# One triangular substitution for a whole pair of heads, and 36 adaLN columns moved from VectorE to GpSimd and ScalarE

## The chip, the cores and the metric

The kernel runs on one core of one Trainium2 chip. The time is device time in microseconds (us), the median of three runs: 2511.28 before (2510.93 to 2513.99). Engines are named as the profile names them: PE (TensorE), PEld (its weight loads), DVE (VectorE), ACT (ScalarE), POOL (GpSimd), SP (SyncE, which issues all transfers here). Each engine has its own list of instructions, in the order in which they were built; semaphores make one engine wait for another.

## What is computed

One decoder layer in float32, batch 1, 512 tokens, width 2048:

```python
mod = silu(c) @ w_ada + b_ada            # 6 x 2048 values: shift, scale, gate of both sub-layers
h = modulate(rms_norm(x), sh_m, sc_m)
p = h @ w_in                             # RG-LRU part, its gate, RWKV part
y_a = rg_lru(conv(p_lru)) * gelu(p_gate)
y_b = rwkv7_mix(p_rwkv)                  # 16 heads of 64; state (64 x 64) per head over all tokens
x = x + g_m * (concat(y_a, y_b) @ w_out)
h = modulate(rms_norm(x), sh_f, sc_f)
x = x + g_f * ((silu(gate) * up) @ w_down)
return rms_norm(x)
```

The RWKV recurrence is worked in 8 chunks of 64 tokens for 8 pairs of heads. Within a chunk it needs, per head, the inverse of a unit triangular 64 x 64 matrix I - A.

## The kernel before

Large products are made of three float32r products each, of operands split into a high and a low part (lines 124 to 126, tiles `whi`, `wlo` of the weights and `hhi`, `hlo` or `yhi`, `ylo` of the activations). A block of weights comes in by SP, ACT casts it to `whi` (L105), DVE makes `wlo` (L106).

The mixing sub-layer is one long stage in which `weave` writes the order of work down once, when the program is built. It has streams of small dependent steps and a `filler` of large products (input projections of later pairs, the RG-LRU, and half of the output projection). It goes by a clock of its own: a stream's next step is placed when its stated latency has passed and what it needs has been placed; else three large products of the filler are placed. What PE does while it waits for a chain of small steps is therefore fixed beforehand, and if the filler is used up, nothing is placed between. The streams, by priority, are

- `chains`: for each pair, 8 chunks one after the other. A chunk's steps are a product (L694, L696), ACT's copy `rw_w` (L698), a product with the inverse `bd_xt` (L701), ACT's copy `rw_u` (L703), products L708 to L713, and DVE's next state `rw_s` (L720). After 8 chunks come group norm and gate (L729 to L745) and a store of the pair's `y`.
- `halves(0)`, `halves(1)`: four chunks of a pair. Operands, products within chunks (L633, L643), DVE's `rw_gb` and `rw_dg` (L635 to L639), transposes on PE (L655), and then `inverse` for these four chunks. A half of pair p is placed once four, or all eight, chunks of pair p-1 are placed.
- `mains`: what a pair needs of all tokens. `mods`: the adaLN columns 32 to 67.

`inverse` does a substitution by DVE in the diagonal 32 x 32 blocks. A transpose spreads `rw_dg` over the partitions (L757, tile `rw_at`), then 31 steps of a multiply (L764, `rw_xp`) and an add (L766, `rw_x`), each on the one before, then two transposes (L768 `rw_xn`, L771 `rw_xs`), and POOL's copies into `bd_xt` (L775). PE then makes the lower left blocks (L783, a copy by ACT, L793). `weave` counts 30.2 us for the substitution. The two halves of a pair have buffers of their own and may be under way together.

`mod_steps` makes an adaLN column in four quarters: SP loads 128 x 512 of `w_ada` (tile `adaq`, two buffers), and one DVE instruction multiplies by the spread silu(c) (`cbq`) and sums along the row (L199).

After the mixing, `channel` loads the eight `y` of the pairs back (`yraw`, two buffers), splits them (`yhi`, `ylo`), and runs the other half of the output projection.

Of the kernel before, what the change touches and what calls it, by code (L numbers as in the profile page):

```python
# [67 lines left out]
def _constants():  # L68
# [9 lines left out]
    r = ((p % 32) // 4)[:, None, None]  # L78
    con[:, _COFF["xinit"]:][:, :P] = (
        np.arange(32)[None, :, None] == 8 * np.arange(4)[None, None, :] + r).reshape(P, P)  # L80
# [965 lines left out]
```

## Time and profile before

| | before |
|---|---|
| median of 3 runs | 2511.28 us |
| span of the profiled execution | 2515.8 us (4.5 above the median; the page gives no other time of it) |
| busy: PE, DVE, ACT, POOL | 2413.9, 1380.4, 843.7, 82.0 us |
| 150 to 850 us (most of the mixing): PE, DVE, ACT busy of 700 | 667.9, 612.9, 374.8 us |
| mean granted PE clock | 0.986 |

The busy time of an engine over the whole span says little here, since the mixing and the later stages have different limits. A stage is read by its window; a wait is read by the pair of engines and lines that it names.

### The profile page before, as it was taken

What the parts mean: (1) busy time and instruction counts of PE and PEld (TensorE: products, weight loads), DVE (VectorE), ACT (ScalarE), POOL (GpSimd) and SP (SyncE); (2) the same over time, 40 slices, a digit from 0 to 9 for tenths busy, and PEclk for the clock granted to TensorE, in tenths of its full rate; (3) what the DMA queues carried; (4) which work ended last, traced back from release to release, by engine and by line L of the source; (5) the groups of instructions that cost most, each with busy time, mean ns of one, the idle gap of its engine ahead of it and who ended that gap; (6) DMA issues with size and microseconds to landing.
All of it is one profiled execution on the core that took longest, in us unless ns stands there. A gap on an engine that the chain in (4) does not pass through costs nothing.

```text
span 2515.8 us, 30983 instructions
## 1 busy us (share of the span) xinstructions
PE 2413.9 (96%) x11560; PEld 1953.4 (78%) x11560; DVE 1380.4 (55%) x3111; ACT 843.7 (34%) x1340; POOL 82.0 (3%) x131
## 2 busy tenths in 40 slices
PE   5999999999999999899999999999999999999997
PEld 3677777877777886687788888888888888888885
DVE  7979898999969847854423322233322233222244
ACT  4357364455355333432222222222222222222221
POOL 0000111111101000000000000000000000000000
PEclk9999998999999999999999999999999999999998
DMA  8864444444342438366423332323333233333233
GB/s 304 308 219 130 148 128 143 131 152 144 125 135 81 143 108 283 119 195 194 160 90 95 108 100 93 101 83 98 106 98 99 89 92 105 101 93 100 85 95 112
DMA packets 138938, 333.22 MB, mean 132 GB/s; under 512 B 15458, under 2 KB 28898, under 8 KB 134690
## 3 DMA queue, kind: packets, MB, share of 16 engines
q1 hardware_dynamic: 138788, 331.25, 40.7%
q8 instruction: 90, 1.47, 0.2%
q14 instruction: 60, 0.49, 0.1%
HBM read 322.92 MB, written 7.87 MB: 131 GB/s over the span
## 4 chain that ended last, share of the span: by engine, by line
PE 72%; DVE 9%; DMA 7%; issue 1%; ACT 1%; SPq 0%; POOL 0%; DVEq 0%; ACTq 0%
PE ps_mm L124 10%; PE ps_mm L126 10%; PE ps_mm L125 10%; PE ps_gr L126 6%; PE ps_st L124 6%; PE ps_gr L124 6%; PE ps_st L126 6%; PE ps_gr L125 6%; PE ps_st L125 6%; DMA adaq<-in_w_ada 6%; DVE adaq L199 2%; DVE wlo L106 2%; DVE rw_xp L764 1%; DVE rw_x L766 1%; DMA wraw<-in_w_out 1%
## 5 line engine op out<-in xcount | busy, mean ns | idle before, releaser
L106 DVE TENSOR_TENSOR wlo<-wraw,whi 128x1024 fp32r<-128x1024 f32 (+2 forms) x552 | 496.7, 902 | 730.2 <-ACT whi L105 721.1
L105 ACT CAST whi<-wraw 128x1024 fp32r<-128x1024 f32 (+2 forms) x552 | 436.6, 792 | 1292.4 <-PE ps_mm L125 401.1
L124 PE MATMUL ps_mm<-hhi,whi 128*128 128x512 f32 x1020 | 417.1, 410 | 9.8 <-ACT hhi L251 7.2
L126 PE MATMUL ps_mm<-hhi,wlo 128*128 128x512 f32 x1020 | 407.2, 399 | 1.7 <-DVE wlo L106 1.6
L125 PE MATMUL ps_mm<-hlo,whi 128*128 128x512 f32 x1020 | 406.5, 399 | 0.8 <-DVE hlo L252 0.7
L124 PEld LDWEIGHTS ps_mm<-hhi,whi 128*128 128x128 f32 x1020 | 193.4, 190 | 53.2 <-ACT hhi L251 9.9
L125 PEld LDWEIGHTS ps_mm<-hlo,whi 128*128 128x128 f32 x1020 | 193.7, 190 | 43.4 <-DVE hlo L252 4.8
L126 PEld LDWEIGHTS ps_mm<-hhi,wlo 128*128 128x128 f32 x1020 | 193.8, 190 | 42.3 <-DVE wlo L106 3.0
L199 DVE SCALAR_TENSOR_TENSOR adaq<-adaq,cbq 128x512 f32<-128x512 f32 x256 | 173.5, 687 | 92.9 <-DMA adaq<-in_w_ada 85.1
L126 PE MATMUL ps_gr<-hhi,wlo 128*128 128x512 f32 x496 | 193.7, 390 | 3.1 <-DVE wlo L106 3.1
L126 PE MATMUL ps_st<-hhi,wlo 128*128 128x512 f32 x496 | 193.6, 390 | 2.0 <-DVE wlo L106 2.0
L124 PE MATMUL ps_st<-hhi,whi 128*128 128x512 f32 x496 | 194.0, 391 | 1.6 <-ACT hhi L251 1.6
L125 PE MATMUL ps_gr<-hlo,whi 128*128 128x512 f32 x496 | 193.5, 390 | 0.0
L125 PE MATMUL ps_st<-hlo,whi 128*128 128x512 f32 x496 | 193.5, 390 | 0.0
L124 PE MATMUL ps_gr<-hhi,whi 128*128 128x512 f32 x496 | 192.6, 391 | 0.0
L126 PEld LDWEIGHTS ps_gr<-hhi,wlo 128*128 128x128 f32 x496 | 93.4, 188 | 23.6 <-DVE wlo L106 4.1
L126 PEld LDWEIGHTS ps_st<-hhi,wlo 128*128 128x128 f32 x496 | 93.4, 188 | 21.8 <-DVE wlo L106 2.5
L124 PEld LDWEIGHTS ps_st<-hhi,whi 128*128 128x128 f32 x496 | 93.5, 188 | 21.6 <-ACT hhi L251 2.2
L125 PEld LDWEIGHTS ps_gr<-hlo,whi 128*128 128x128 f32 x496 | 93.7, 189 | 19.6
L124 PEld LDWEIGHTS ps_gr<-hhi,whi 128*128 128x128 f32 x496 | 93.7, 189 | 19.4
L125 PEld LDWEIGHTS ps_st<-hlo,whi 128*128 128x128 f32 x496 | 93.3, 188 | 19.8 <-DVE hlo L252 0.3
L766 DVE TENSOR_TENSOR rw_x<-rw_x,rw_xp 128x27 f32<-128x27 f32 (+23 forms) x496 | 94.7, 196 | 5.7
(312 smaller groups left out, 3809.6 us busy)
## 6 DMA issues: line engine op xcount, KB each, us to landing
wraw<-in_w_gu SPq DMA_DIRECT2D x176, 512.0 KB, 3.6
adaq<-in_w_ada SPq DMA_DIRECT2D x256, 256.0 KB, 3.3
wraw<-in_w_in SPq DMA_DIRECT2D x160, 256.0 KB, 3.0
ada<-in_w_ada SPq DMA_DIRECT2D x32, 1024.0 KB, 7.2
wraw<-in_w_down SPq DMA_DIRECT2D x64, 512.0 KB, 3.5
wraw<-in_w_out SPq DMA_DIRECT2D x64, 256.0 KB, 3.3
wraw<-in_w_down SPq DMA_DIRECT2D x64, 192.0 KB, 2.3
x<-in_x SPq DMA_DIRECT2D x32, 256.0 KB, 5.3
```

The lines of the kernel that those rows point to most:

```text
L105: nc.scalar.copy(out=hi, in_=src)
L106: nc.vector.tensor_tensor(out=lo, in0=src, in1=hi.bitcast(F32), op=ALU.subtract)
L124: mm(ps, lhsT=w[0], rhs=x[0], start=start, stop=False)
L125: mm(ps, lhsT=w[0], rhs=x[1], start=False, stop=False)
L126: self.pe = mm(ps, lhsT=w[1], rhs=x[0], start=False, stop=stop).ins
L199: nc.vector.scalar_tensor_tensor(out=t, in0=t, scalar=1.0, in1=cb, op0=ALU.mult, op1=ALU.mult, accum_out=part[:, m, h:h + 1])
L764: tt(out=pr[:, :n, :j], in0=at[:, s + 1:, s:s + 1].to_broadcast([P, n, j]), in1=x[:, s:s + 1, :j].to_broadcast([P, n, j]), op=ALU.mult)
L766: tt(out=x[:, s + 1:, :j], in0=x[:, s + 1:, :j], in1=pr[:, :n, :j], op=ALU.add)
```

## The change

Per pair there is now one substitution for all eight chunks, in a stream `inverses` of its own, placed when both halves of the pair are built; its tiles hold twice the columns, and there is one buffer of each. `weave` counts 24.0 us for it. The chain of a pair starts when that one inverse is placed. The adaLN columns 32 to 67 (144 quarters) go through `mod_steps_pool`: POOL multiplies (L224), ACT sums along the row one quarter later (L215), and `adaq` has three buffers. Comments were taken out, which shifts the line numbers.

```diff
-INVLAT = 30.2                   # substitution in the diagonal blocks
+INVLAT = 24.0
...
+    def mod_steps_pool(self, js, pool, tags):
+        nc = self.nc
+        n = len(js)
+        part = self.small.tile([P, n, 4], F32, tag="adaparts", name="adaparts", bufs=1)
+        old = None
+
+        def total(t, at):
+            nc.scalar.activation(out=t, in_=t, func=AF.Copy, accum_out=at)
+
+        for h in range(4):
+            sl = slice(h * S, (h + 1) * S)
+            cb = pool.tile([P, S], F32, tag=tags[0], name="cbq", bufs=tags[1])
+            nc.sync.dma_start(out=cb, in_=self.csilu[:, sl].to_broadcast([P, S]))
+            for m, j in enumerate(js):
+                t = pool.tile([P, S], F32, tag=tags[2], name="adaq", bufs=tags[3])
+                nc.sync.dma_start(out=t, in_=self.i["w_ada"][j, :, sl])
+                nc.gpsimd.tensor_tensor(out=t, in0=t, in1=cb, op=ALU.mult)
+                if old is not None:
+                    total(*old)
+                old = t, part[:, m, h:h + 1]
+                yield
+        total(*old)
...
-                for _ in self.mod_steps(range(j, min(j + 16, 64 + 4)), self.rw, ("cbq", 1, "adaq", 2)):
+                for _ in self.mod_steps_pool(range(j, min(j + 16, 64 + 4)), self.rw, ("cbq", 1, "adaq", 3)):
...
+        def inverses():
+            for pr in range(NPAIR):
+                yield 0, 0, lambda: done["built"] == 2 * pr + 2
+                yield from self.inverse(*self.pairs[pr][-1])
+
         def chains():
             for pr in range(NPAIR):
-                yield 0, 0, lambda: done["inv"] > 2 * pr
+                yield 0, 0, lambda: done["inv"] > pr
                 yield from self.rwkv_chain(pr)
...
-        self.weave([chains(), halves(0), halves(1), mains(), mods()], self.filler)
+        self.weave([chains(), inverses(), halves(0), halves(1), mains(), mods()], self.filler)
...
-            if c == 4:
-                yield 0, 0, lambda: self.done["inv"] >= 2 * pr + 2
...
-        yield from self.inverse(hf, d, gb)
...
-        at = rw.tile([P, 32, 32], F32, tag=f"at{hf}", name="rw_at")
+        at = rw.tile([P, 32, 32], F32, tag="at", name="rw_at")
...
-        x = rw.tile([P, 32, 4], F32, tag=f"x{hf}", name="rw_x")
+        x = rw.tile([P, 32, 8], F32, tag="x", name="rw_x")
...
-            n, j = 31 - s, s // 8 + 1
+            n, j = 31 - s, s // 4 + 1
             tt(out=pr[:, :n, :j], in0=at[:, s + 1:, s:s + 1].to_broadcast([P, n, j]),
```

What now stands where, by the built order of both programs:

On PE, the place of the last substitution that PE uses. Before, in pair 7's second half (L783 is the product that takes `rw_xn`; `ps_mm<-yhi` are large products of the filler):

```order
L712 MATMUL ps_y<-rw_ar,rw_s 128x64
L713 MATMUL ps_y<-rw_gb,rw_u 128x64
L783 MATMUL ps_gr<-rw_xn,rw_gb 32x32 x8
L124 MATMUL ps_mm<-yhi,whi 128x512
L125 MATMUL ps_mm<-ylo,whi 128x512
L126 MATMUL ps_mm<-yhi,wlo 128x512
```

In the change (L783 is now L816, L793 is L826, the transposes L655 are L690, the chain's L701 and L709 are L733 and L741):

```order
L126 MATMUL ps_mm<-yhi,wlo 128x512
L657 MATMUL ps_st<-cons,mix_v 64x64 x8
L666 MATMUL ps_gr<-rw_ar,bd_b_1390 128x128 x4
L678 MATMUL ps_gr<-rw_ar,bd_k_1392 128x128 x4
L775 MATMUL ps_ch<-lora_g,rw_lwg 128x512
L776 MATMUL ps_ch<-lora_s,rw_lws 128x512
L690 MATMUL ps_st<-cons,bd_b_1390 128x128 x4
L726 MATMUL ps_ch<-bd_v_1402,bd_bt_1398 128x128
L690 MATMUL ps_st<-cons,bd_k_1392 128x128 x4
L742 MATMUL ps_y<-rw_rkt,bd_v_1402 128x64
L816 MATMUL ps_gr<-rw_xn,rw_gb 32x32 x16
L826 MATMUL ps_gr<-rw_xs,rw_rt 32x32 x16
```

The first of these rows is the filler's last product. From there to the end of pair 7's chain and its group norm no large product stands on PE; before, 273 of them stood between the last transposes L655 and the end of the filler, and the chain of pair 7 had ended 39 before it. Between the second half's last transposes and the substitution's first use, PE has 125, 116, 133, 112, 130, 123, 130 and 0 large products for pairs 0 to 7 (before, for the 16 halves, 96 to 181); on DVE there stand 101 to 111 rows of the order from the last `rw_dg` to `rw_xn` for pairs 0 to 6, of which 62 are the substitution and 9 to 12 are `wlo`.

On POOL, pair 2's second half to pair 2's copies of the inverse (L616 is now L649, L775 is L807). Before, with nothing else between:

```order
L616 TENSOR_SCALAR bd_a_1394<-rw_ar 64x4x64 x2
L775 TENSOR_SCALAR bd_xt_1407<-rw_xs 32x4x32 x4
L616 TENSOR_SCALAR bd_a_1395<-rw_ar 64x4x64 x2
L554 MEMSET rw_pb 128x8
L775 TENSOR_SCALAR bd_xt_1406<-rw_xs 32x4x32 x4
```

In the change:

```order
L649 TENSOR_SCALAR bd_a_1394<-rw_ar 64x4x64 x2
L224 TENSOR_TENSOR adaq<-adaq,cbq 128x512 x16
L649 TENSOR_SCALAR bd_a_1395<-rw_ar 64x4x64 x2
L587 MEMSET rw_pb 128x8
L224 TENSOR_TENSOR adaq<-adaq,cbq 128x512 x25
L807 TENSOR_SCALAR bd_xt_1406<-rw_xs 32x4x32 x4
L807 TENSOR_SCALAR bd_xt_1407<-rw_xs 32x4x32 x4
```

In the same stretch of pairs 0, 1 and 3 there are 18, 16 and 12 of these multiplies, and from pair 4 on none.

On ACT, from pair 7's last square (`L729`, now `L761`) to the projection. Before:

```order
L729 ACTIVATE rw_t_9389<-ps_y 128x512
L105 CAST whi<-wraw 128x512 x2
L735 ACTIVATE rw_t_9434<-ps_ch,eps 128x512
L736 ACTIVATE rw_t_9389<-rw_t_9434 128x512
L105 CAST whi<-wraw 128x512 x4
L105 CAST yhi<-yraw 128x512 x2
L105 CAST whi<-wraw 128x512
```

In the change:

```order
L761 ACTIVATE rw_t_9018<-ps_y 128x512
L767 ACTIVATE rw_t_9022<-ps_ch,eps 128x512
L768 ACTIVATE rw_t_9018<-rw_t_9022 128x512
L105 CAST yhi<-yraw 128x512 x4
L105 CAST whi<-wraw 128x512 x2
L105 CAST yhi<-yraw 128x512 x4
```

The casts of filler weights are gone from between, and the first weights that the projection needs are cast behind four `yhi`.

More of the change, by code (lines that the diff above doesn't have):

```diff
@@ L77, in _constants @@
     con[:, _COFF["gmask"] + C:][:, :C] = s <= t
[L78 to L80 removed]
+    r = ((p % 32) // 8)[:, None, None]
+    con[:, _COFF["xinit"]:][:, :256] = (
+        np.arange(32)[None, :, None] == 4 * np.arange(8)[None, None, :] + r).reshape(P, 256)
     q = (p // 32) % 2
@@ L201, in mod_steps @@
                 yield
+        dst = self.mod[:, js[0]:js[0] + n]
+        nc.vector.tensor_reduce(out=dst, in_=part, op=ALU.add, axis=AX.X)
+        o = _VOFF["b_ada"] + js[0]
+        nc.vector.tensor_tensor(out=dst, in0=dst, in1=self.vecs[:, o:o + n], op=ALU.add)
+    def mod_steps_pool(self, js, pool, tags):
[18 more added lines that the diff above has]
+        total(*old)
         dst = self.mod[:, js[0]:js[0] + n]
@@ L635, in rwkv_half @@
         tt(out=gb, in0=pv, in1=gm.unsqueeze(1).to_broadcast([P, 4, P]), op=ALU.mult)
-        d = rw.tile([P, 4, 32], F32, tag=f"dg{hf}", name="rw_dg")
+        if hf == 0:
+            parts.append(rw.tile([P, NCH, 32], F32, tag="dg", name="rw_dg"))
+        d = parts[0][:, 4 * hf:4 * hf + 4]
         nc.vector.tensor_scalar(out=d, in0=gb[:, :, 0:32], scalar1=self.m01[:, 0:1], scalar2=None,
@@ L748, in rwkv_chain, with inverse @@
         yield 1.07, 2.0, None
-    def inverse(self, hf, dg, gb):
+    def inverse(self, dg, *parts):
         nc, rw = self.nc, self.rw
@@ L766, in inverse @@
             tt(out=x[:, s + 1:, :j], in0=x[:, s + 1:, :j], in1=pr[:, :n, :j], op=ALU.add)
-        xn = rw.tile([P, 32, 4], F32, tag=f"at{hf}", name="rw_xn")
-        nc.vector.transpose(out=xn.rearrange("p (j r) c -> p j (r c)", r=8),
+        xn = rw.tile([P, 32, NCH], F32, tag="at", name="rw_xn")
+        nc.vector.transpose(out=xn.rearrange("p (j r) c -> p j (r c)", r=4),
                             in_=x.rearrange("p t j -> p j t"))
-        xs = rw.tile([P, 4, 32], F32, tag=f"dg{hf}", name="rw_xs")
+        xs = rw.tile([P, NCH, 32], F32, tag="xp", name="rw_xs")
         nc.vector.transpose(out=xs, in_=xn.rearrange("p j c -> p c j"))
-        xt = self.bd["xt"][hf]
-        for g in range(4):
-            rows = slice(g * 32, g * 32 + 32)
-            nc.gpsimd.tensor_scalar(out=xt[rows, :, rows], in0=xs[rows], scalar1=1.0,
-                                    scalar2=None, op0=ALU.mult)
+        for hf in range(2):
+            for g in range(4):
+                rows = slice(g * 32, g * 32 + 32)
+                nc.gpsimd.tensor_scalar(out=self.bd["xt"][hf][rows, :, rows], in0=xs[rows, 4 * hf:4 * hf + 4],
+                                        scalar1=1.0, scalar2=None, op0=ALU.mult)
         yield 0, INVLAT, None
-        ps = self.ps("gr").rearrange("p (c x) -> p c x", x=P)
-        for c in range(4):
+        ps = self.ps("gr").rearrange("p (c x) -> p c x", x=C)
+        for c in range(NCH):
+            gb = parts[c // 4][1]
             for g in range(2):
                 q0, q1 = slice(g * C, g * C + 32), slice(g * C + 32, g * C + C)
-                mm(ps[q1, c, :32], lhsT=gb[q0, c, 32:C], rhs=xn[q0, :, c], start=True, stop=True)
-        rt = rw.tile([P, 4, 32], F32, tag=f"x{hf}", name="rw_rt")
+                mm(ps[q1, c, :32], lhsT=gb[q0, c % 4, 32:C], rhs=xn[q0, :, c], start=True, stop=True)
+        rt = rw.tile([P, NCH, 32], F32, tag="x", name="rw_rt")
         for g in range(2):
@@ L787, in inverse @@
             nc.scalar.copy(out=rt[q1], in_=ps[q1, :, :32])
-        yield 0.43, HOP, None
-        ps = self.ps("gr").rearrange("p (c x) -> p c x", x=P)
-        for c in range(4):
+        yield 0.86, HOP, None
+        ps = self.ps("gr").rearrange("p (c x) -> p c x", x=C)
+        for c in range(NCH):
             for g in range(2):
@@ L793, in inverse @@
                 mm(ps[q0, c, :32], lhsT=rt[q1, c, :], rhs=xs[q1, c, :], start=True, stop=True)
-        for g in range(2):
-            q0, q1 = slice(g * C, g * C + 32), slice(g * C + 32, g * C + C)
-            nc.scalar.copy(out=xt[q0, :, q1], in_=ps[q0, :, :32])
-        yield 0.43, 1.4, None
+        for hf in range(2):
+            for g in range(2):
+                q0, q1 = slice(g * C, g * C + 32), slice(g * C + 32, g * C + C)
+                nc.scalar.copy(out=self.bd["xt"][hf][q0, :, q1], in_=ps[q0, 4 * hf:4 * hf + 4, :32])
+        yield 0.86, 1.4, None
         self.done["inv"] += 1
```

10 lines of the change are left out of this document (5 added, 5 removed).

## Prediction

> **What bounds it now.** I read the page's engine rows and slices first, then the mixing by windows, then PE's waits, then single stretches of the timeline. In the fence: the page's rows (busy us, share, instructions), three windows (length, busy us and count of PE, PEld, DVE, ACT, POOL, then the granted PE clock, DMA share, GB/s), and the largest row of PE's waits (sum, times, longest).
>
> ```profile
> PE 2413.9 (96%) x11560; PEld 1953.4 (78%) x11560; DVE 1380.4 (55%) x3111; ACT 843.7 (34%) x1340; POOL 82.0 (3%) x131
> PE   5999999999999999899999999999999999999997
> 150.00:850.00 700.00, 667.90 (x3851) 531.13 (x3850) 612.91 (x1962) 374.79 (x705) 76.32 (x116) 0.97 0.43 136
> 893.00:920.00 27.00, 27.00 (x163) 22.98 (x161) 7.69 (x13) 7.68 (x20) 0.00 (x0) 1.00 0.22 64
> 932.00:955.00 23.00, 19.45 (x79) 14.16 (x78) 10.42 (x16) 7.89 (x13) 0.00 (x0) 1.00 0.80 265
> PE ps_gr L783 <- DVE rw_xn L768: 18.7, 8, 3.7
> ```
>
> PE is the bound almost everywhere, so the change can earn only what PE loses in the mixing: 32.1 us idle in 150 to 850 us, of which 18.7 us are eight waits for the substitution, and time at a lowered clock. The last two windows show what covers pair 7's chain of chunks today: PE has large products throughout, and it loses only 3.5 us while the `y` are read back. That cover is what I look at most.
>
> One of the eight waits, PE's timeline (start, length), and the first and last of the seven stretches that begin with such a wait and have the clock at half:
>
> ```profile
> 428.90 0.39 PE L124 MATMUL ps_mm<-hhi,whi 128*128 128x512 f32 x1
> 429.13 0.39 PE L125 MATMUL ps_mm<-hlo,whi 128*128 128x512 f32 x1
> 433.23 0.66 PE L783 MATMUL ps_gr<-rw_xn,rw_gb 32*32 32x32 f32 x16 [3.71 <-DVE rw_xn L768]
> 434.41 0.63 PE L124 MATMUL ps_mm<-hhi,whi 128*128 128x512 f32 x1
> 434.84 0.63 PE L125 MATMUL ps_mm<-hlo,whi 128*128 128x512 f32 x1
> 347.20:350.60 3.40, 3.40 (x10) 2.75 (x10) 2.07 (x5) 1.18 (x4) 0.84 (x2) 0.50 0.26 98
> 432.60:442.70 10.10, 9.47 (x49) 6.01 (x50) 6.05 (x24) 6.64 (x12) 2.84 (x4) 0.50 0.46 145
> 715.90:722.60 6.70, 6.12 (x43) 4.59 (x44) 3.49 (x9) 2.89 (x6) 2.37 (x4) 0.50 0.69 201
> ```
>
> Large products start 0.23 us apart at full clock and 0.43 us apart after the wait. The seven stretches add up to about 40 us; nearly half of that, 18.6 us (40 x 0.2/0.43), is lost. So the substitution costs 18.7 + 18.6 = 37 us today.
>
> **Part 1, what the new order uncovers.** By the order, the filler is used up before pair 7's second half is finished: its products, its substitution, the chain of eight chunks and the group norm have no large product between. I sum their length alone from rows of this trace. Substitution (first its transpose in, two dependent steps, the last steps and the transpose out):
>
> ```profile
> 857.93 2.05 DVE L757 STREAM_TRANSPOSE rw_at<-rw_dg 128x1024 f32<-128x1024 f32 x1
> 870.60 0.20 DVE L764 TENSOR_TENSOR rw_xp<-rw_at,rw_x 128x40 f32<-128x40 f32 x1
> 870.83 0.20 DVE L766 TENSOR_TENSOR rw_x<-rw_x,rw_xp 128x40 f32<-128x40 f32 x1
> 881.52 0.16 DVE L764 TENSOR_TENSOR rw_xp<-rw_at,rw_x 128x4 f32<-128x4 f32 x1
> 881.72 0.16 DVE L766 TENSOR_TENSOR rw_x<-rw_x,rw_xp 128x4 f32<-128x4 f32 x1
> 881.92 0.40 DVE L768 STREAM_TRANSPOSE rw_xn<-rw_x 128x128 f32<-128x128 f32 x1
> ```
>
> Steps start 0.23 us apart at 40 elements and 0.20 at 4, about 0.001 us an element. The new steps hold 8 to 76, on average 50 (30 before), so 62 x 0.245 = 15.2 us; with 2.05 in, some 0.65 out and 3.4 us of pair 6's group norm, which the order puts between, 21 us. Building the half up to `rw_dg` comes before it, 4 us. The lower left blocks, twice as many, with ACT's copies: 4 us. So the first chunk can use the inverse 29 us after the last large product of the filler. A chunk's round and the end of a chain:
>
> ```profile
> 913.17 0.39 PE L709 MATMUL ps_ch<-rw_u,rw_bn 128*128 128x128 f32 x2
> 914.42 0.34 DVE L720 SCALAR_TENSOR_TENSOR rw_s<-ps_ch,rw_pcs,rw_w 128x128 f32<-128x128 f32 x1
> 916.37 0.39 PE L696 MATMUL ps_ch<-rw_s,bd_a 128*128 128x128 f32 x2
> 916.85 0.27 ACT L698 COPY rw_w<-ps_ch 128x128 f32<-128x128 f32 x1 [3.32 <-PE ps_ch L696]
> 917.98 0.39 PE L701 MATMUL ps_ch<-rw_w,bd_xt 128*128 128x128 f32 x2
> 918.40 0.27 ACT L703 COPY rw_u<-ps_ch 128x128 f32<-128x128 f32 x1 [0.52 <-PE ps_ch L701]
> 924.72 0.69 ACT L735 ACTIVATE rw_t<-ps_ch,eps 128x512 f32<-128x512 f32 x1 [0.42 <-PE ps_ch L732]
> 930.78 0.69 DVE L745 TENSOR_TENSOR rw_t<-rw_t,ps_ch 128x512 f32<-128x512 f32 x1
> ```
>
> The six instructions of a round take 2.05 us and each hands on 0.05 to 0.15 us later: 2.6 us, or 3.4 us with PE at half clock. I take 3.0, and 22 us for eight (the first and the last are shorter). From the last product to L745 without the casts between: 7.5 us (L735 to L745 alone is 6.8 above). Then `y` goes out and the eight come back through two buffers:
>
> ```profile
> 931.50 0.33 SPq L746 DMA_DIRECT2D y<-rw_t  x1
> 934.24 0.80 SPq L439 DMA_DIRECT2D yraw<-y  x2
> 937.80 1.29 DVE L106 TENSOR_TENSOR ylo<-yraw,yhi 128x512 fp32r<-128x512 f32 x2
> 938.51 0.93 SPq L439 DMA_DIRECT2D yraw<-y  x2
> 943.18 1.36 DVE L106 TENSOR_TENSOR ylo<-yraw,yhi 128x512 fp32r<-128x512 f32 x2 [2.35 <-ACT yhi L105]
> ```
>
> A pair of loads takes 4.9 us from issue to both `ylo` (934.24 to 939.09) and the next pair is issued as the first gets split. On ACT the projection's first weights are cast behind four `yhi`, so PE's first large product waits for two pairs: 11 us behind L745. Sum: 29 + 22 + 7.5 + 11 = 69.5 us. PE's own small products in it (some 6 for the half, 2 for the blocks, 1.7 a chunk, 2 at the end: 24 us) are paid today too. Remain 45.5; plus 3 us for weights whose loads now stand behind all eight `yraw` in SP's order and 2.5 us of half clock on resuming, less the 3.5 us idle of today's window and about 2.4 us of what follows: **+45 us**. Bounds: 35 (round 2.6, `yraw` already overlapped) and 55 (round 3.4, `yraw` pairs one after the other).
>
> **Part 2, the substitution in the seven earlier pairs.** PE has 112 to 133 large products between, 26 to 31 us at 0.23, and 4 us of small ones. DVE needs 15.2 + 2.7 us for the substitution, 10 x 0.6 for `wlo`, and some 30 others at 0.4 to 0.5: 36 to 39 us, though it starts about 2 us before PE's last transposes end. Left for PE: a wait of 2 us and, as in the rows above, a 3.4 us stretch at half clock that costs 1.6: 7 x 3.6 = 25 us. Removing 144 DVE instructions and half of the steps does not clear it, because the shorter 24.0 us also takes PE's work away.
>
> POOL's multiplies add to this. One two-input multiply of 128 x 512 is not in the trace; the nearest rows are POOL's one-input copy and DVE beside it. The first row gives all 32 copies (minimum, median, maximum in ns), the last the group that moves off DVE (busy, mean ns, idle time before it):
>
> ```profile
> L616 POOL TENSOR_SCALAR bd_a<-rw_ar x32: 844/990/1830, 213.4 to 849.4; 64x256 f32<-64x256 f32 x32
> 410.50 2.51 POOL L616 TENSOR_SCALAR bd_a<-rw_ar 64x256 f32<-64x256 f32 x2 [23.12 <-DVE rw_ar L609]
> 410.86 0.39 DVE L766 TENSOR_TENSOR rw_x<-rw_x,rw_xp 128x36 f32<-128x36 f32 x1
> 411.62 0.68 DVE L199 SCALAR_TENSOR_TENSOR adaq<-adaq,cbq 128x512 f32<-128x512 f32 x1
> 412.23 0.38 DVE L766 TENSOR_TENSOR rw_x<-rw_x,rw_xp 128x34 f32<-128x34 f32 x1
> L199 DVE SCALAR_TENSOR_TENSOR adaq<-adaq,cbq 128x512 f32<-128x512 f32 x256 | 173.5, 687 | 92.9 <-DMA adaq<-in_w_ada 85.1
> ```
>
> Each of the two POOL instructions delays one DVE step by 0.2 us (0.39 instead of 0.20), while L199, which also reads two tiles, runs beside them at its usual length. A multiply reads four times as many elements per partition (2 x 512 against 256): 0.2 to 0.8 us. 71 of them stand in the stretches of pairs 0 to 3; at 0.3 they add 21 us, at 0.8 57 us. In the trace a POOL instruction takes 1.25 us here, so a multiply is 1.3 to 3.4 us; at four times 1.25, 144 would take 490 of some 600 us, so POOL itself is no bound. ACT's 144 sums, at the 0.69 of L735 some 100 us over those 600 us, hide in its idle 325 of 700; if they delay the chain's copies, up to 10 us more. Together 25 + 21 = 46 us against today's 37: **+9 us**, between -25 and +45.
>
> On the port there is a rule that speaks against the change: the Trainium skill, SBUF — State Buffer, Who interferes with whom, says a DVE instruction with two SBUF inputs and a GpSimd instruction that reads SBUF exclude each other for the whole instruction. The 0.68 us of L199 beside POOL does not look like that; it is the second rival below.
>
> **Sum:** the profiled execution has a span of 2515.8 us, 4.5 above the median 2511.3 of the runs, and its rows give the terms: 2515.8 + 45 + 9 = 2570, less 4.5 for a median of runs, **2565 us**.
>
> **Rivals.**
> (a) The relief works: DVE is ready before PE in all seven pairs. For it: DVE loses 144 of the 256 L199 of 0.687 us, 99 us, and half of the steps; against: the shorter planned time. 37 us are gained instead of 9 lost: 2511 + 45 - 37 = 2519.
> (b) POOL holds DVE off for its whole instruction, and ACT's sums, which wait for POOL, hold the casts behind them. For it: POOL's 1.25 us against an undisturbed 0.85 or so suggests that the two take turns; against: the 0.2 us above. 71 x 1.7 (two undisturbed instructions) x 0.8 (DVE's share of two-input work) = 97 instead of 21: 2565 + 76 = 2640.
> (c) Not slower: with DVE relieved, PE's other waits in 150 to 850 us (13 us) go too, and the uncovered end is at its lower bound: 2511 - 37 - 13 + 35 = 2496. It decides once the end costs less than the 50 us that can be won. Against it: the end alone is 35 at the least, so nearly every wait must go.
> (d) The adaLN columns finish late and the gate keeps the filler back, which moves cover to the end: the end costs half, 2540. Little speaks for it, as they end by pair 3 in the order.
>
> **Chances.** Forecast 0.62, (a) 0.14, (b) 0.13, (c) 0.07, (d) 0.04. The forecast's own range is 2530 to 2605. What a measurement of this kernel can tell from no change is about 0.2%, 5 us. Below 2506 lie (c) and a little of (a): 0.08. Within 5 us part of (a): 0.05. Slower 0.87. The range takes in (a): 2519 to 2608.
>
> **What would show it.** Right: after the filler's last product (about 880 to 900 us) a stretch of some 70 us in which PE is busy about 24, DVE first and then ACT, PE and DVE in turn; half clock after it; the row L816 <- L800 among PE's waits with 10 to 50 us; DVE steps longer in pairs 0 to 3 than later. Wrong: large products beside pair 7's chain; no wait at L816; or DVE steps of 1 us and more beside POOL.

## The result

The changed kernel takes **2635.2 us** (median of 4 runs, 2634.1 to 2645.9) against 2511.9 us of the kernel before: **1.050 times as long, 95% interval 1.048 to 1.052**, 123 us more. The prediction had the direction, but 54 of the 123 us: 2565, with a range that ended at 2608. Its second rival, 2640 by a lock between GpSimd and VectorE, came out within 5 us of the time.

### The profile page after: what moved, and what is told of

It reads as the page before. It is cut to its first block, busy times and chain, and to the rows that moved or that the text cites. A ratio compares the mean times of both kernels' runs of the same rounds, so it can differ in the third digit from the quotient of the medians.

```text
span 2643.7 us, 30720 instructions
## 1 busy us (share of the span) xinstructions
PE 2448.1 (93%) x11560; PEld 1982.0 (75%) x11560; DVE 1320.7 (50%) x2295; ACT 932.9 (35%) x1610; POOL 271.2 (10%) x275
## 4 chain that ended last, share of the span: by engine, by line
PE 68%; DVE 13%; DMA 7%; ACT 2%; issue 2%; POOL 1%; SPq 0%; DVEq 0%; POOLq 0%; ACTq 0%
PE ps_mm L124 9%; PE ps_mm L125 9%; PE ps_mm L126 9%; PE ps_gr L124 6%; PE ps_gr L126 6%; PE ps_gr L125 6%; PE ps_st L124 6%; PE ps_st L125 6%; PE ps_st L126 6%; DMA adaq<-in_w_ada 5%; DVE wlo L106 3%; DVE rw_xp L796 2%; DVE rw_x L798 2%; DVE adaq L199 1%; POOL adaq L224 1%
## 5 line engine op out<-in xcount | busy, mean ns | idle before, releaser
L106 DVE TENSOR_TENSOR wlo<-wraw,whi 128x512 fp32r<-128x512 f32 (+2 forms) x552 | 513.4, 932 | 808.7 <-ACT whi L105 774.4
L105 ACT CAST whi<-wraw 128x512 fp32r<-128x512 f32 (+2 forms) x552 | 436.5, 792 | 1270.4 <-PE ps_mm L125 375.9
L124 PE MATMUL ps_mm<-hhi,whi 128*128 128x512 f32 x1020 | 419.9, 413 | 12.5 <-ACT hhi L279 7.1
L126 PE MATMUL ps_mm<-hhi,wlo 128*128 128x512 f32 x1020 | 411.4, 403 | 1.8 <-DVE wlo L106 1.7
L124 PEld LDWEIGHTS ps_mm<-hhi,whi 128*128 128x128 f32 x1020 | 196.3, 193 | 59.4 <-issue 10.7
L126 PEld LDWEIGHTS ps_mm<-hhi,wlo 128*128 128x128 f32 x1020 | 196.6, 193 | 47.9 <-DVE wlo L106 4.5
L224 POOL TENSOR_TENSOR adaq<-adaq,cbq 128x512 f32<-128x512 f32 x144 | 197.9, 1390 | 189.9 <-DMA adaq<-in_w_ada 118.8
L124 PE MATMUL ps_st<-hhi,whi 128*128 128x512 f32 x496 | 194.0, 391 | 1.6 <-ACT hhi L279 1.6
L126 PE MATMUL ps_st<-hhi,wlo 128*128 128x512 f32 x496 | 193.7, 390 | 1.6 <-DVE wlo L106 1.6
L126 PE MATMUL ps_gr<-hhi,wlo 128*128 128x512 f32 x496 | 193.3, 390 | 1.8 <-DVE wlo L106 1.8
L124 PE MATMUL ps_gr<-hhi,whi 128*128 128x512 f32 x496 | 192.4, 391 | 0.0
L215 ACT ACTIVATE adaq<-adaq 128x512 f32<-128x512 f32 x144 | 90.4, 628 | 89.1 <-POOL adaq L224 87.5
L199 DVE SCALAR_TENSOR_TENSOR adaq<-adaq,cbq 128x512 f32<-128x512 f32 x112 | 75.1, 689 | 74.4 <-DMA adaq<-in_w_ada 70.5
L124 PEld LDWEIGHTS ps_st<-hhi,whi 128*128 128x128 f32 x496 | 93.5, 188 | 21.6 <-ACT hhi L279 2.2
L126 PEld LDWEIGHTS ps_gr<-hhi,wlo 128*128 128x128 f32 x496 | 93.2, 188 | 21.9 <-DVE wlo L106 2.3
L126 PEld LDWEIGHTS ps_st<-hhi,wlo 128*128 128x128 f32 x496 | 93.4, 188 | 21.7 <-DVE wlo L106 2.4
L124 PEld LDWEIGHTS ps_gr<-hhi,whi 128*128 128x128 f32 x496 | 93.7, 189 | 19.4
```

The costliest lines, as they stand in the source:

```text
L105: nc.scalar.copy(out=hi, in_=src)
L106: nc.vector.tensor_tensor(out=lo, in0=src, in1=hi.bitcast(F32), op=ALU.subtract)
L124: mm(ps, lhsT=w[0], rhs=x[0], start=start, stop=False)
L126: self.pe = mm(ps, lhsT=w[1], rhs=x[0], start=False, stop=stop).ins
L199: nc.vector.scalar_tensor_tensor(out=t, in0=t, scalar=1.0, in1=cb, op0=ALU.mult, op1=ALU.mult, accum_out=part[:, m, h:h + 1])
L215: nc.scalar.activation(out=t, in_=t, func=AF.Copy, accum_out=at)
```

## The profile after

The page of the changed kernel: the engines' busy time, and in 40 slices the busy tenths of PE and POOL and the granted clock.

```profile
PE 2448.1 (93%) x11560; PEld 1982.0 (75%) x11560; DVE 1320.7 (50%) x2295; ACT 932.9 (35%) x1610; POOL 271.2 (10%) x275
PE   6988797878999995889999999999999999999997
POOL 0013546553011010000000000000000000000000
PEclk9999898988999995989999999999999999999998
```

There are two dents in PE where the kernel before had 9s: counted from 0, a shallow one over slices 2 to 9, just where POOL is busy, and a deep one in slice 15. Two windows show them, the first of them also for the kernel before (length, busy us and count of PE, PEld, DVE, ACT, POOL, granted clock, DMA share, GB/s). First the kernel before, then the changed one:

```profile
190.00:650.00 460.00, 439.07 (x2542) 348.30 (x2541) 419.30 (x1365) 245.42 (x458) 47.96 (x71) 0.96 0.44 137
```

```profile
190.00:650.00 460.00, 376.23 (x1953) 293.36 (x1954) 335.35 (x625) 293.71 (x645) 227.33 (x195) 0.90 0.46 144
989.10:1062.50 73.40, 41.38 (x235) 33.91 (x233) 30.10 (x94) 13.52 (x40) 4.18 (x8) 0.58 0.07 22
```

From 190 to 650 us PE is busy 63 us less, at a lower clock, although DVE is busy 84 us less. Between 989.1 and 1062.5 us no large product starts: this is pair 7's end, as predicted. PE's small products fill 41.4 us there at a mean clock of 0.58, or some 24 us at full speed, so the pause loses 73.4 - 24 = **49 us**.

The rest follows from counting the large products (the rows of L124 to L126 in order of start). Number 2600 (counted from 0), just behind the mixing, starts at 957.3 us before and at 1080.4 us after, 123 us later. 49 of them are the pause; **74 us were lost earlier**, in the weave of pairs 0 to 6. Another 5 us come behind it: the two profiled executions lie 128 us apart (spans of 2515.8 and 2643.7), the medians 123. The same count is used for the experiments below.

PE's waits changed their place too (the largest rows; sum, times, longest):

```profile
PE ps_st L620 <- DVE rw_t L617: 31.1, 8, 8.7
PE ps_gr L816 <- DVE rw_xn L800: 30.4, 7, 19.4
PE ps_st L601 <- ACT rw_t L599: 11.9, 6, 3.8
PE ps_mm L124 <- DMA yraw<-y: 9.4, 1, 9.4
PE ps_ch L733 <- ACT rw_w L730: 9.2, 6, 3.2
```

The substitution (L816) takes 19.4 us of its 30.4 at pair 7, and only 11 us in the seven pairs before, less than the 18.7 us it had. The new loss is in front of other steps of pairs 0 to 3, which wait for DVE and ACT in general. Why DVE is late shows in its timeline, once beside GpSimd's multiplies (changed kernel, DVE's rows, then POOL's):

```profile
415.98 0.18 DVE L798 TENSOR_TENSOR rw_x<-rw_x,rw_xp 128x24 f32<-128x24 f32 x1
416.19 0.17 DVE L796 TENSOR_TENSOR rw_xp<-rw_at,rw_x 128x16 f32<-128x16 f32 x1
416.40 1.15 DVE L798 TENSOR_TENSOR rw_x<-rw_x,rw_xp 128x16 f32<-128x16 f32 x1
417.58 1.18 DVE L796 TENSOR_TENSOR rw_xp<-rw_at,rw_x 128x8 f32<-128x8 f32 x1
418.80 1.18 DVE L798 TENSOR_TENSOR rw_x<-rw_x,rw_xp 128x8 f32<-128x8 f32 x1
420.01 0.63 DVE L800 STREAM_TRANSPOSE rw_xn<-rw_x 128x256 f32<-128x256 f32 x1
...
416.25 3.71 POOL L224 TENSOR_TENSOR adaq<-adaq,cbq 128x512 f32<-128x512 f32 x3 [4.81 <-DMA cbq<-csilu]
```

A step of 0.17 us takes 1.15 to 1.18 us: each of the three ends when one of the three multiplies (3.71 us together, 1.24 each) ends. Here the two engines take turns by whole instructions. All 30 steps of the substitution that a multiply held in this trace ended 0.02 to 0.09 us behind the end of that multiply. Over the trace I compared each DVE instruction that overlaps a multiply with the median of the same form alone: the lengthening adds up to **84 us**, 0.58 us for each of the 144 multiplies; ACT's instructions beside them kept their length (297 of them, less than 1 us in sum). A second candidate stands beside it, ACT's waits between 190 and 650 us:

```profile
ACT adaq L215 <- POOL adaq L224: 87.5, 74, 4.9
```

ACT stood 87.5 us in 74 waits for a multiply, with casts and copies of the chain queued behind. Which of the two cost the 74 us, the traces alone cannot say.

## Experiments

Two theories: **port**, the multiplies hold DVE's instructions and so make all that hangs on them late; **queue**, an in-order engine (ACT, or GpSimd itself) stands still at a column's instruction with other work behind it. Times are medians. "Lengthening" is the sum described above, of that kernel's trace.

### The two halves of the change apart

e1, the substitution alone:

```diff
-                for _ in self.mod_steps_pool(range(j, min(j + 16, 64 + 4)), self.rw, ("cbq", 1, "adaq", 3)):
+                for _ in self.mod_steps(range(j, min(j + 16, 64 + 4)), self.rw, ("cbq", 1, "adaq", 2)):
```

> The changed kernel with the adaLN columns of the mixing back on DVE (L199's form, two buffers): the one substitution alone. In the changed kernel's trace the large products pause for 73 us at pair 7, where PE has some 24 us of small products, about +50 us; the other 74 of the +123 us were lost earlier, in pairs 0 to 3. Theory A (the columns on GpSimd and ScalarE cost the 74): the pause stays, the 74 go, 2555 to 2575. Theory B (the substitution and its new order cost the 74, the columns little): about 2635. Theory C (DVE needs the relief, so the columns on it make the 0.2 us steps wait): above 2600 with the waits of PE for the substitution at 40 us and more.

Measured: **2563.4 us, 1.0198 (1.0181 to 1.0215)**. The pause is there (909.7 to 978.5 us, 68.8 us long, 45 lost), large product 2600 starts at 996.7 us, so the weave is 5 us better than before; another 7 us are lost behind that product. Theory A.

e2b, the columns alone: the kernel before with the changed kernel's `mod_steps_pool`, called with two buffers. With three, as the change has, there was no room: the pool of the RG-LRU needs 18.06 KB per partition and 16.06 were left, so that kernel has no time.

> The kernel before with the adaLN columns of the mixing on GpSimd and ScalarE (two buffers for the quarters, as it had), and its two substitutions a pair as they were. If the columns cost what the changed kernel and the one with the substitution alone differ by, 72 us, whatever the substitution: 2512 + 72 = 2584, up to 2610 since 62 more two-input steps a pair can meet a multiply. If the columns cost only beside the long substitution of eight chunks: below 2550.

Measured: **2606.7 us, 1.0370 (1.0349 to 1.0391)**. No pause, and 92 us lost by large product 2600, as the first theory has it; lengthening 103 us, since two substitutions a pair offer the multiplies more steps to hold. So the columns cost 72 us (2635.2 - 2563.4) on the new substitution and some 92 on the old one, and the substitution by itself costs 49 us, all of it in pair 7's pause and behind it.

### Taking the multiply or its consumer away

e4 drops the multiply; e5 keeps it, but lets nobody wait for it:

```diff
-                nc.gpsimd.tensor_tensor(out=t, in0=t, in1=cb, op=ALU.mult)
```

```diff
-            cb = pool.tile([P, S], F32, tag=tags[0], name="cbq", bufs=tags[1])
-            nc.sync.dma_start(out=cb, in_=self.csilu[:, sl].to_broadcast([P, S]))
+            cb = pool.tile([P, S], BF16, tag=tags[0], name="cbq", bufs=tags[1])
+            cu = pool.tile([P, S], BF16, tag="scu", name="scu", bufs=1)
...
-            nc.scalar.activation(out=t, in_=t, func=AF.Copy, accum_out=at)
+            nc.scalar.activation(out=cu, in_=t, func=AF.Copy, accum_out=at)
...
-                nc.gpsimd.tensor_tensor(out=t, in0=t, in1=cb, op=ALU.mult)
+                nc.gpsimd.tensor_tensor(out=cb, in0=t, in1=t, op=ALU.mult)
```

> The changed kernel without the multiply on GpSimd: ScalarE sums each quarter as loaded (the factor silu(c) is left out of these columns). ScalarE's 144 sums and the loads stay. Theory port (the multiplies hold DVE's two-input steps: in the changed kernel's trace 84 us of lengthened DVE instructions): most of the 74 us go, 2560 to 2580. Theory queue (ScalarE's casts and copies stand behind sums that wait, 87.5 us in 74 waits there, and GpSimd itself waited 119 us for the loads, which ScalarE now waits for): 2610 to 2635.

> The changed kernel with GpSimd multiplying each loaded quarter by itself into a 16-bit scratch tile that nobody reads, while ScalarE sums the quarter as loaded into another scratch tile (the product with silu(c) is left out, and its four broadcast loads): the multiplies are there, but ScalarE waits for none of them. Theory port: DVE's steps are held as before, 2615 to 2635. Theory queue through GpSimd: 2570 to 2590. If this one and the one without the multiply both stay high, ScalarE's wait for the loads is the cause.

Measured: e4 **2544.6 us, 1.0128 (1.0108 to 1.0148)**, below the expected span; e5 **2601.5 us, 1.0346 (1.0324 to 1.0367)**, between the expectations. The multiply is worth 2635.2 - 2544.6 = 91 us. In e5 the multiply had become shorter, 1.15 us on average instead of 1.39, and the lengthening smaller, 48 us instead of 84, so its 34 us less than the changed kernel could be either theory's. It settled nothing by itself.

e8 writes each sum one quarter later still, e9 leaves the sums out and the columns zero (parts of the two edits):

```diff
-                if old is not None:
-                    total(*old)
-                old = t, part[:, m, h:h + 1]
+                if len(old) == 2:
+                    total(*old.pop(0))
+                old.append((t, part[:, m, h:h + 1]))
...
```

```diff
-                if old is not None:
-                    total(*old)
-                old = t, part[:, m, h:h + 1]
...
-        total(*old)
```

> The changed kernel whole, with each of ScalarE's sums written one column later (two multiplies behind instead of one, the same three buffers). GpSimd's multiplies and their 1.39 us stay, so DVE's lengthening should stay near 84 us. Theory queue (ScalarE standing still behind GpSimd costs 30 us and more by itself): 2595 to 2610, with ScalarE's wait for GpSimd at half of the 87.5 us or less. Theory port alone (the 34 us between the changed kernel and the one where nobody waits came from its shorter multiply, 1.15 us, and 36 us less of lengthened DVE steps): 2625 to 2640.

> The changed kernel without ScalarE's 144 sums: GpSimd multiplies in place, and nothing reads the product (these columns are left zero). The price of the multiplies on DVE's port alone, at their own length. Theory port: the 2545 of the kernel without the multiply, plus some 60, less up to 5 for ScalarE's missing sums: 2595 to 2610, and DVE's lengthening at 70 to 90 us. Theory queue: 2550 to 2570.

Measured: e8 **2634.8 us, 1.0495 (1.0474 to 1.0515)**, but ACT's wait for GpSimd did not fall (91.8 us in 72 waits; SP still waited 103 us for the buffers that ACT frees, 105 in the changed kernel, so the loads came no earlier), so it did not change what it was meant to change. e9 **2641.4 us, 1.0522 (1.0504 to 1.0541)**: with no sum at all, and so no wait of ACT for a multiply, the whole loss stays, with 83 us of lengthening. It even lies above both expectations. ACT's queue is not needed for the loss. The window from 190 to 650 us of e9:

```profile
190.00:650.00 460.00, 373.61 (x1969) 294.27 (x1968) 332.20 (x630) 201.18 (x358) 227.75 (x195) 0.89 0.46 144
```

PE is busy 373.6 us, 2.6 less than in the changed kernel, and DVE as busy as there.

### One input instead of two

e7 keeps everything but the second input of GpSimd's instruction; e10 is e7 without the sums, e11 is e9 without the multiply:

```diff
-                nc.gpsimd.tensor_tensor(out=t, in0=t, in1=cb, op=ALU.mult)
+                nc.gpsimd.tensor_scalar(out=t, in0=t, scalar1=1.0, scalar2=None, op0=ALU.mult)
```

> The changed kernel with GpSimd's instruction made one-input: the loaded quarter times 1.0 in place, the same tile and count, ScalarE's sums waiting for it as before (the factor silu(c) is left out). Theory inputs (what holds DVE is GpSimd's second SBUF input; the prediction's 0.2 us came from one-input copies): DVE's lengthening is some 20 us instead of 84, ScalarE's wait stays, so 2545 + 34 = 2580, between 2560 and 2590. Theory any (every GpSimd instruction of this length holds DVE): 2620 to 2640.

> The kernel with GpSimd's one-input instruction, without ScalarE's sums (these columns are left zero). If the sums' wait behind GpSimd is what costs there beyond the port: 2592 falls to 2560 to 2570 (2545 and the 19 us of lengthened DVE steps). If GpSimd's own occupation or the loads behind it cost: 2585 to 2600.

> The loads of the columns alone: no multiply and no sum (the columns are left zero). The sums beside free GpSimd then cost what the 2545 of the kernel without the multiply lies above this one. If ScalarE's 90 us of sums hide, as the prediction had it: 2540 to 2546. If they delay casts and copies by themselves: 2525 to 2535.

| GpSimd's instruction | with ACT's sums | without | lengthening (with, without) |
|---|---|---|---|
| none | 2544.6 | 2553.7 | 0, 0 |
| one-input, 1.49 us | 2592.1 | 2609.3 | 19, 22 us |
| two-input, 1.30 us (medians of one) | 2635.2 | 2641.4 | 84, 83 us |

(Ratios to the kernel before: e7 1.0310, 1.0287 to 1.0333; e10 1.0389, 1.0374 to 1.0405; e11 1.0171, 1.0154 to 1.0188.) Down each column the time rises from no instruction to one input to two; across each row the sums cost nothing on balance. Without them each kernel is 6 to 17 us slower. The traces have a likely reason in a third in-order queue, SP's, where the loads of weights stand behind loads of columns that wait for a buffer. From 190 to 650 us, ACT's casts in e9 wait for weights:

```profile
ACT whi L105 <- DMA wraw<-in_w_in: 31.2, 7, 7.4
```

In e10 and e11 this row has 35.1 and 20.9 us, in e4 and e7 0.5, and the changed kernel has no such row. So late weights belong to the kernels without sums, and are no part of what the multiplies cost with them; how much of the 6 to 17 us they make, no run shows. The second input alone is worth 43 us with the sums and 32 us without. e7 and e11 are above their expected ranges, e10 above the higher of its two: a one-input instruction costs 47 to 56 us, more than its lengthening of some 20. Its rows show a short hold, as the prediction had read it from the kernel before (e7, DVE, then POOL):

```profile
373.83 0.22 DVE L796 TENSOR_TENSOR rw_xp<-rw_at,rw_x 128x64 f32<-128x64 f32 x1
374.08 0.57 DVE L798 TENSOR_TENSOR rw_x<-rw_x,rw_xp 128x64 f32<-128x64 f32 x1
374.68 0.24 DVE L796 TENSOR_TENSOR rw_xp<-rw_at,rw_x 128x75 f32<-128x75 f32 x1
374.96 0.24 DVE L798 TENSOR_TENSOR rw_x<-rw_x,rw_xp 128x75 f32<-128x75 f32 x1
375.24 0.24 DVE L796 TENSOR_TENSOR rw_xp<-rw_at,rw_x 128x70 f32<-128x70 f32 x1
...
373.96 1.49 POOL L224 TENSOR_SCALAR adaq<-adaq 128x512 f32<-128x512 f32 x1 [6.86 <-DMA adaq<-in_w_ada]
```

The step that meets the beginning of GpSimd's instruction ends 0.69 us after that beginning (374.65); the next two run at full speed within it. Over e7's trace, 21 steps of the substitution were held; each was 0.29 to 0.45 us longer and ended 0.80 us or a little more before the end of GpSimd's instruction, and the 66 others that began beside one kept their length. The groups of the window 190 to 650 us say the same: the mean ns of one step and of one `wlo` (the number behind the busy time), in the changed kernel, in e7 and in e4.

```profile
L798 DVE TENSOR_TENSOR rw_x<-rw_x,rw_xp 128x60 f32<-128x60 f32 (+24 forms) x118 | 40.7, 345 | 2.4
L106 DVE TENSOR_TENSOR wlo<-wraw,whi 128x512 fp32r<-128x512 f32 x87 | 76.0, 873 | 61.4 <-ACT whi L105 44.0 <-PE ps_ch L741 9.3 <-PE ps_mm L126 5.0
L647 DVE TENSOR_TENSOR bd_b<-rw_a,rw_pi 64x256 f32<-64x256 f32 x16 | 14.8, 925 | 0.2
```

```profile
L798 DVE TENSOR_TENSOR rw_x<-rw_x,rw_xp 128x60 f32<-128x60 f32 (+24 forms) x124 | 29.4, 237 | 2.5
L106 DVE TENSOR_TENSOR wlo<-wraw,whi 128x512 fp32r<-128x512 f32 x96 | 69.4, 723 | 81.7 <-ACT whi L105 72.9 <-PE ps_ch L741 2.8 <-PE ps_mm L126 2.5
```

```profile
L797 DVE TENSOR_TENSOR rw_x<-rw_x,rw_xp 128x60 f32<-128x60 f32 (+24 forms) x143 | 30.8, 215 | 2.9
L106 DVE TENSOR_TENSOR wlo<-wraw,whi 128x512 fp32r<-128x512 f32 x109 | 75.0, 688 | 80.1 <-ACT whi L105 65.4 <-PE ps_ch L740 7.7 <-PE ps_ch L727 3.2
```

Not only the substitution is held: `wlo`, which every large product needs, goes from 688 to 873 ns, and the operand `bd_b` takes 925 ns, against 486 in e7 and 415 in e4.

### GpSimd's own queue

What else does the one-input instruction cost? The copies into `bd_a` and `bd_xt` and two memsets stand behind it on GpSimd. Three kernels put them on other engines: f4 without the multiply, f7 one-input, fA the changed kernel.

```diff
-            nc.gpsimd.tensor_scalar(out=ba[rows, :, cols], in0=ar[rows, :, :C], scalar1=1.0,
-                                    scalar2=None, op0=ALU.mult)
+            nc.scalar.copy(out=ba[rows, :, cols], in_=ar[rows, :, :C])
...
-                nc.gpsimd.tensor_scalar(out=self.bd["xt"][hf][rows, :, rows], in0=xs[rows, 4 * hf:4 * hf + 4],
-                                        scalar1=1.0, scalar2=None, op0=ALU.mult)
+                nc.scalar.copy(out=self.bd["xt"][hf][rows, :, rows], in_=xs[rows, 4 * hf:4 * hf + 4])
...
-        nc.gpsimd.memset(pb[:, :, 0:1], 1.0)
+        nc.vector.memset(pb[:, :, 0:1], 1.0)
...
-            nc.gpsimd.memset(th[:, 0:1], 1.0)
+            nc.vector.memset(th[:, 0:1], 1.0)
```

> The kernel without the multiply (2545), with the copies into bd_a and bd_xt on ScalarE and the two memsets of the mixing on DVE, so that GpSimd does nothing in the weave: the base for its two siblings. ScalarE is busy 334 of 460 us there, so 2540 to 2560.

> The same moves in the kernel with GpSimd's one-input instruction (2592): nothing stands behind it on GpSimd any more. If GpSimd's own queue made the rest of the 47 us: 15 to 25 us above its base. If not (the port, or the loads and buffers): 40 us and more above it.

> The same moves in the changed kernel (2635). If GpSimd's queue bears a part of its 91 us over the kernel without the multiply: 60 to 75 us above the base. If the port bears all: 85 to 95 us above it.

Measured: f4 2549.3 us (1.0155, 1.0131 to 1.0179), f7 2585.5 (1.0301, 1.0283 to 1.0319), fA 2630.5 (1.0486, 1.0467 to 1.0505). Over f4 that is 36 us for the one-input and 81 us for the two-input instruction, instead of 47 and 91: GpSimd's own queue bears about 10 us of either, between the two expectations both times, and no better known than that, since f4's runs spread from 2542 to 2555 us. The lengthening (22 and 81 us) stays. So of the 91 us of the multiply some 80 remain without that queue, as much as the lengthening of DVE's instructions; such a match is rough (103 us of lengthening for 92 in e2b, 48 for 57 in e5). In f7, 14 us beyond the 22 us of lengthened instructions remain; that PE's lowered clock after each wait and a later `wlo` make them is likely from the rows, but no run shows it, and it stays open.

### Covering pair 7's end

If the pause is lost cover and nothing else, other work behind it must bring it back. v1 is e1 with products of the first six of the eight rwkv blocks of the output projection as additional filler, so that only two are left behind the mixing, and with the 12 columns 68 to 79 made in the mixing too (their planned latency 5.0 instead of 2.0):

```diff
             yield from self.project(self.ya, 1, "mm")
+            yield lambda: done["out"] >= 6
+            self.yc = [self.load_y(k, self.big) for k in range(8, 14)]
+            yield from self.project(self.yc, 0, "mm", n0=0)
...
-            for j in range(32, 64 + 4, 16):
-                for _ in self.mod_steps(range(j, min(j + 16, 64 + 4)), self.rw, ("cbq", 1, "adaq", 2)):
+            for j in range(32, 80, 16):
+                for _ in self.mod_steps(range(j, j + 16), self.rw, ("cbq", 1, "adaq", 2)):
...
-            yield from self.gemm_steps(p, self.i["w_out"][half, m], ys)
+            yield from self.gemm_steps(p, self.i["w_out"][half, m][:, n0 * P:], ys)
```

> The one substitution with the columns on DVE (2563), with work behind which pair 7's end can lie: the first six of the eight rwkv halves' rows of the output projection (288 large products, 65 us) become filler behind the first half, and the last 12 adaLN columns before the channel sub-layer are made in the mixing too. Theory A (the pause of 69 us at pair 7 is lost cover alone, some 45 us of it): the pause goes, 2510 to 2520. Theory B (the pause only changes place: the chain's steps grow longer between large products, or the casts for the additional products are late): 2535 to 2560.

Measured: **2520.8 us, 1.0028 (1.0016 to 1.0041)**, 42.6 us less than e1, theory A but for 1 us. Pair 7's chain now has large products beside it (window of v1):

```profile
950.00:1000.00 50.00, 49.70 (x304) 42.52 (x304) 17.37 (x34) 16.27 (x46) 3.68 (x8) 1.00 0.20 61
```

v3 gives the kernel before 192 additional products of filler, made in the same way, and a longer planned substitution (`INVLAT` 34.0 instead of 30.2). v4 is v1 with the last `y` split on chip instead of going out and back:

```diff
-        nc.sync.dma_start(out=self.ydram[8 + pr], in_=y)
+        if pr < NPAIR - 1:
+            nc.sync.dma_start(out=self.ydram[8 + pr], in_=y)
+        else:
+            self.y15 = (self.big.tile([P, S], F32R, tag="h", name="yhi"),
+                        self.big.tile([P, S], F32R, tag="h", name="ylo"))
+            self.split_into(*self.y15, y)
```

> The kernel before with four of the rwkv row blocks of the output projection (192 large products, 44 us) as additional filler, the last 12 adaLN columns made in the mixing, and the planner's latency of the substitution 34.0 instead of 30.2. If PE's waits in the mixing (32 us idle, some 19 at half clock) come from a latency set too short: 20 to 35 us faster, 2477 to 2492. If DVE's load sets them, so that later steps are late as well: 2500 to 2515.

> The version with the additional cover (2521), in which the last pair's y is split on chip instead of going out and back, and the y of the pair before it is loaded at the end of the filler. After the last large product of the filler that version pauses 13.8 us, 9.9 of them PE's wait for the two casts of this y. Theory A (the way out and back is that wait): 9 us less, 2510 to 2514. Theory B (the casts are late because ScalarE and VectorE are, not the transfer): 2517 to 2522.

Measured: v3 **2521.4 us, 1.0028 (1.0014 to 1.0043)**, slower than the kernel before by 0.3%, above both expectations. PE's wait for the substitution is still 13.6 us there. Up to large product 2100 v3 is 11 us ahead of the kernel before; it loses this at a stop of 9.9 us from 809.7 us on, where PE waits for another of DVE's steps (L587). Since v3 has the additional filler and columns too, it does not tell how much of the waits a latency set too short makes. v4 **2514.8 us, 1.0006 (0.9994 to 1.0019)**: 6 of the expected 9 us, and no difference from the kernel before. The one substitution, with its end covered, shows neither a gain nor a loss: v1 and v3, which both have additional filler and columns, take the same time.

v5 and v6 go by the planner's numbers: v5 is v4 with head 3's gelu branch ahead of pair 7's products and `INVLAT` 20.0, v6 is v5 with head 2's branch too ahead of its pair's products, `HOP` 0.95 and `LSN` 1.40.

> The same with two more edits to the order: head 3's gelu branch stands ahead of pair 7's key, value and receptance products in the filler, and the planner's latency of the substitution is 20.0 instead of 24.0. In the version with the additional cover the filler stands still at 1968 large products until pair 5 is built: 9.3 and 5.6 us with no large product, at half clock behind. If that standstill is the filler's gate: some 10 us less than the sibling without these edits, 2500 to 2505. If the shorter latency only turns cover into waits for the substitution (11 us there now): 2510 to 2520, with that wait at 20 us and more.

> As the one with the other order, head 2's gelu branch too ahead of its pair's products, and the planner's latencies of a small product and of the next state 0.95 and 1.40 instead of 1.10 and 1.79 (a round of the chain took 2.6 us alone at pair 7, and the planner allows some 4). If the planner allows too much: 5 us less than its sibling, 2495 to 2500. If steps of the chain wait behind casts on ScalarE and so need what it allows: no gain or 5 to 10 us more, 2505 to 2515.

Measured: 2529.0 us (1.0070, 1.0048 to 1.0092) and 2528.5 us (1.0066, 1.0050 to 1.0083). Both lie above every span that was expected. In v5 the standstill at the 1968th product is gone, but its trace has five others (5.5 to 7.8 us, between 305 and 804 us), and 10.1 us of waiting for the substitution, about as before (11.3 in v4). What makes v5 14 us slower than v4 is not shown. No version here beats the kernel before.

## Why the prediction was wrong, step by step

**What bounds it.** PE, right. The cover of pair 7's chain was the place to look at, and the loss there came as told.

**Part 1, the uncovered end: right in sum (+45 foretold, 35 to 55; 49 measured in the pause, +49 for e1 by itself, 42.6 given back by cover in v1, 48.6 in v4, which also spares the last `y` its way out and back), though partly by luck.** Its terms, from the changed kernel's rows:

```profile
1014.92 1.15 PE L816 MATMUL ps_gr<-rw_xn,rw_gb 32*32 32x32 f32 x32 [19.37 <-DVE rw_xn L800]
1018.69 0.77 PE L733 MATMUL ps_ch<-rw_w,bd_xt 128*128 128x128 f32 x2 [0.70 <-ACT bd_xt L830]
1022.72 0.80 PE L733 MATMUL ps_ch<-rw_w,bd_xt 128*128 128x128 f32 x2
1048.71 0.60 ACT L761 ACTIVATE rw_t<-ps_y 128x512 f32<-128x512 f32 x1 [0.78 <-PE ps_y L745]
1056.22 0.69 DVE L777 TENSOR_TENSOR rw_t<-rw_t,ps_ch 128x512 f32<-128x512 f32 x1
1062.46 0.80 PE L124 MATMUL ps_mm<-yhi,whi 128*128 128x512 f32 x1 [9.38 <-DMA yraw<-y]
```

The window of the eight rounds (length, busy us and count of PE, PEld, DVE, ACT, POOL, granted clock, DMA share, GB/s):

```profile
1018.70:1048.70 30.00, 29.23 (x116) 25.90 (x116) 2.46 (x7) 6.17 (x23) 1.45 (x3) 0.50 0.00 1
```

From 989.1 us to the first use of the inverse it is 29.6 us (29 foretold), eight rounds take 30.0 (22 foretold), the tail to the end of L777 8.2 (7.5), the `y` 5.5 (11). Two terms were off and nearly cancel, which is luck. A round takes some 4.0 us, not 3.0: the clock stands at 0.50 in all eight. The three products of a round take 0.80, 0.80 and 0.74 us there instead of 0.39, and one of them (L728) stands 0.5 us behind other products of the round, because PE has a product in progress for 29.2 of the 30.0 us. The bound of 3.4 us "with PE at half clock" was summed too low, for three products of 0.39 us doubled add 1.2 to 2.6. Why the clock stays at half while PE has work is not shown. The `y` came after one pair of loads, not two.

**Part 2, the substitution in the earlier pairs: about right.** 25 us against today's 37 were foretold, 12 less. Without the columns' multiplies the weave is 5 us better than before with the columns on DVE (e1) and 20 us with DVE relieved of them (e4: product 2600 at 982.4 us, its pause 68.8 us long).

**Part 2, POOL's multiplies: this step failed, and by itself it makes the miss.** It took "0.2 to 0.8 us" for a multiply from a one-input copy, "0.3" of it as the value, and "71" multiplies that count: 21 us. The trace shows 0.58 us on average over all 144, 84 us, and the kernel pays 91 for the multiplies: 70 more than the 21, and the whole miss is 70 (2635 - 2565). Two things were wrong. The row was of the wrong kind: the copy of 64 partitions x 256 has one input, and at the multiply's own size an instruction with one input holds DVE for its first part only (e7, 19 us of lengthening), one with two inputs for its whole length (the changed kernel, 84 us). And not only the substitution's steps meet the multiplies; `wlo`, `bd_b` and `bd_k` do as well. The upper bound of the estimate (0.8 for 71, 57 us) was too low for the second reason, and the range ended below the result with it. A check beside it was also summed wrong, without consequence: "at four times 1.25" the 144 multiplies would take 720 us, not 490 (that is 144 x 3.4); they took 198.

On this the Trainium skill was the better guide: SBUF — State Buffer, Who interferes with whom, says that a VectorE instruction with two SBUF inputs and a GpSimd instruction that reads SBUF exclude each other for the whole instruction. For the two-input multiply the trace agrees (1.15 to 1.18 us for a step of 0.17 beside multiplies of 1.24); for a one-input instruction it does not (0.69 us of 1.49). The 0.68 us of L199 beside POOL, by which the prediction set the rule aside, was beside such one-input copies, and it met the beginning of neither: L199 began 1.12 us behind the first copy's (1.15 us long) and 0.12 us before the second's.

**The rivals.** (b) had the mechanism, the hold for a whole instruction, and came near in its time (2640 for 2635) and its port part (97 us, measured 84 of lengthening and 91 in time). That the number fits so well is luck: it is 71 multiplies at 1.36 us each, and the trace has 144 at 0.58. Its other half, ACT's sums holding the casts, was real as a wait (87.5 us) and cost nothing on balance (2544.6 us with sums, 2553.7 without; 2635.2 and 2641.4). That ACT hides the sums was the prediction's own term, and right. (a) and (c) fell with the 11 us that stay at L816 and with the multiplies. (d) did not occur: the last multiply begins at 643 us, and the pause has its full length.

**What was to be seen.** The pause, the half clock, L816's wait and the longer steps in pairs 0 to 3 are all there (in the pause PE is busy 41 us, which is the foretold 24 at full clock); so is "DVE steps of 1 us and more beside POOL", which the prediction had named as a sign that it was wrong.

## What to carry to other kernels

Price an instruction on a shared path by a row of the same kind, with the same number of inputs, not by the nearest one scaled by size; where a rule says more than such a row, test the rule's case on the chip or let the range hold it. Moving 0.69 us of VectorE work to GpSimd was no relief here, where much of VectorE's other work reads two tiles: each 1.3 us multiply took 0.58 us of VectorE's time back and put it in front of steps that other engines wait for. Before a chain is made one longer step, count the filler that is left at the last repetition; the end that it uncovers (49 us here) is outside the loop one looks at.
